# A hybrid decoder step on one core: keys of dilated attention gathered by GpSimd, reciprocal roots as one GpSimd power

## Chip, cores and metric

The kernel runs on one core of one Trainium2 chip. The metric is the device time of one execution in microseconds (us). The engines are called PE (TensorE matmuls; PEld is its weight loads), DVE (VectorE), ACT (ScalarE), POOL (GpSimd) and SP (SyncE, which here issues most DMAs).

## The reference

One layer of a decoder with two mixers side by side, for a prompt of 2048 tokens and for 8 x 8 new tokens ("samples") with cached keys and values. Mixer A is a gated MLP over chunks of 128 positions; mixer B is attention over 8 heads of 64 with three dilated patterns: window 128 with step 1, window 512 with step 4, window 2048 with step 16. The three are mixed by their denominators.

```python
def rms_norm(x, g):
    return x * lax.rsqrt(jnp.mean(x * x, axis=-1, keepdims=True) + EPS) * g

PATTERNS = ((128, 1), (512, 4), (2048, 16))
# project: h = rms_norm(x, g_norm); u, va, za, q, k, vb, zb = split(h @ w_in)
# q, k = rms_norm per head
# dilated_prompt_pattern: query t attends to t - j*r, j = 0..n; keys regrouped into
# r residue classes, blocks of 128 queries against own and previous block of 128 keys
s = jnp.einsum('brnqhd,brnkhd->brnhqk', qb, kb) * SCALE
p = jnp.exp(s - m); o = jnp.einsum('brnhqk,brnkhd->brnqhd', p, vb) / p.sum(-1)
# finish: branches normalised, gated, concatenated, @ w_out, + x; then a gated,
# normalised per-layer embedding is added
```

Every RMS norm needs a reciprocal root per row (per row and head or group in the mixers).

## The kernel before

All products are made in f16 with each operand split in a high and a low half. Eight chunks of the input projection run one after the other in the order A0, B0, B1, A1, B2, B3, A2, A3 (`order`, in the main loop); each takes 16 tiles of 128 tokens and one tile of 64 sample tokens. A tile is one `gemm` (L441): 24 matmuls of 128 x 384 (A) or 128 x 512 (B) columns. Four tiles make a group. `b_evac`/`a_evac` empty the result from PSUM, `b_norm`/`a_norm` normalize a group, with its multiplications on POOL (L500 to L513, L581 and L582).

For a group of mixer B, `b_trans` (L533 to L551) then splits queries and keys of a head pair into halves, and DMA transposes on SP put them into `qk2`, one tile per head pair of 6 x 2048 columns: 64 dimensions times two halves on the 128 partitions. Before, the query blocks hold the high half over the low half, and the keys stand there twice, as high over high (`KH`) and low over low (`KL`).

`attn` queues the units of a head pair. In a group of 512 tokens pattern 1 has four units (one block of 128 queries each) and pattern 2 has four (one residue class each); pattern 3 comes after the fourth group and has eight units of two classes. So a head pair has 40 units. A unit's first half is `scores`: matmuls of 128 queries against 256 keys (128 where there is no previous block) for two heads, twice each (L698 with `KH`, L699 with `KL`); DVE adds the mask and takes the maximum (L704), ACT takes the exponential (L712), DVE splits the result (L715, L716), and a DMA transpose (L718) makes `pT`. Its second half, `stage_c`, multiplies `pT` with the values (L739 to L741). For patterns 2 and 3 queries and keys are slices of `qk2` with a step of 4 and 16 columns, `slice(c + s, T, 16)` for instance: both the stationary operand (queries) and the moving one (keys) are read with that step.

`Pump` spreads the units between the matmuls of `gemm`: it counts time by a cost per matmul and per unit (`scores` returns 4 x blocks x (keys x 0.416 + 8) ns) and releases a unit when the count allows. After that the tile framework orders each engine's instructions by its own estimate of times. Each engine works through its list in order. When a head pair is done, `combine` mixes the three patterns, with ten multiplications and additions on POOL per group of 512 tokens. After the chunks the last stage (`p3_out`, `p3_h`, `p3_gate`, `p3_ple`) makes the outputs tile by tile, and the attention of the samples (`sample`) runs beside it; it multiplies cached keys on POOL (L1126), which wait for loads from the cache.

`rsqrt` (L179 to L191) makes all reciprocal roots: eight DVE instructions, a start value from the bits and two polynomial steps. It is called 115 times, on 1, 4, 8 or 16 columns. Calls stand in `xnorm` (the rows of x, before the first projection), `b_norm`, `a_norm`, `a_mix`, `combine`, `p3_ple`, `sample` and `prep_qk`.

Of the kernel before, what the change touches and what calls it, by code (L numbers as in the profile page):

```python
# [11 lines left out]
F16 = mybir.dt.float16  # L12
F32 = mybir.dt.float32
# [8 lines left out]
P = 128  # L22
# [113 lines left out]
def tile_hymba_gmlp_dilated_attn_step(  # L136
# [42 lines left out]
    def rsqrt(src, n, p=P, mul=1.0):  # L179

        y = small(n, f"rsy{n}")[:p]
        t = small(n, f"rst{n}", 2)[:p]
        nc.vector.tensor_scalar(y.bitcast(I32), src.bitcast(I32), -0.5, MAGIC, op0=ALU.mult, op1=ALU.add)
        nc.vector.tensor_tensor(t, y, y, op=ALU.mult)
        nc.vector.tensor_tensor(t, t, src, op=ALU.mult)
        nc.vector.scalar_tensor_tensor(t, t, -10.0 / 3.0, t, op0=ALU.add, op1=ALU.mult)
        nc.vector.scalar_tensor_tensor(y, t, 5.0, y, op0=ALU.add, op1=ALU.mult)
        nc.vector.tensor_tensor(t, y, y, op=ALU.mult)
        nc.vector.scalar_tensor_tensor(t, t, -0.5 * 0.375 ** 3 * mul, src, op0=ALU.mult, op1=ALU.mult)
        nc.vector.scalar_tensor_tensor(y, t, 1.5 * 0.375 * mul, y, op0=ALU.add, op1=ALU.mult)  # L190
        return y  # L191

    def scales(sg, low):

        sgs = small(1, "sgs")
        nc.vector.tensor_scalar(sgs, sg, 1e-30, None, op0=ALU.max)
        e = small(1, "sge").bitcast(I32)
        nc.vector.tensor_scalar(e, sgs.bitcast(I32), -(2.0 ** -24), MAGIC * 2.0 ** -23, op0=ALU.mult, op1=ALU.add)
        y = small(2, "sgy")
# [11 lines left out]
    ones = cst.tile([P, P], F32, name="ones")  # L211
    nc.gpsimd.memset(ones, 1.0)
    nc.scalar.activation(small(1), ones[:, 0:1], AF.Square)
    mask = cst.tile([P, 2, P], BF16, name="mask")
# [49 lines left out]
    def allsum(col):  # L264
        pt = pst("o", 2)
        nc.tensor.matmul(pt[:, 0:1], lhsT=ones, rhs=col, start=True, stop=True)
        return pt[:, 0:1]
# [65 lines left out]
    def wprep(kind, i, fast=False, room=None):  # L333
# [40 lines left out]
        nc.vector.tensor_scalar(sc[:, 4:5], sc[:, 3:4], VS * VS, None, op0=ALU.mult)  # L374
        yield 0.0
# [24 lines left out]
    def xnorm(j, *behind_):  # L400
# [92 lines left out]
    def b_norm(G, sc, gch):  # L493
# [3 lines left out]
        nc.vector.tensor_scalar(ms[:m, :4 * n], G["ss"][:m, :4 * n], 1.0 / HD, sc[:m, 3:4], op0=ALU.mult, op1=ALU.add)  # L497
        y = rsqrt(ms[:m, :4 * n], 4 * n, m, 2.0 ** 12)
# [33 lines left out]
    def b_trans(G):  # L532
# [3 lines left out]
        for q0 in (0, 2):  # L536

            qkc = wk.tile([P, 2, 768], F16, name=nm("qkc"), tag="hl", bufs=2)
            qv = qkc[:, :, 0:256].rearrange("p j (h c d) -> p j h c d", h=2, c=2)
            k_h = qkc[:, :, 256:512].rearrange("p j (h c d) -> p j h c d", h=2, c=2)  # L540
            k_l = qkc[:, :, 512:768].rearrange("p j (h c d) -> p j h c d", h=2, c=2)
            for q in range(2):
                qs, ks = raw[:, q0 + q, 0], raw[:, q0 + q, 1]
                kd_ = ks.unsqueeze(2).to_broadcast([P, 2, 2, HD])
                nc.scalar.activation(qv[:, q, :, 0, :], qs, AF.Copy)
                nc.scalar.activation(k_h[:, q], kd_, AF.Copy)
                nc.vector.tensor_tensor(qv[:, q, :, 1, :], qs, qv[:, q, :, 0, :], op=ALU.subtract)
                nc.vector.tensor_tensor(k_l[:, q], kd_, k_h[:, q], op=ALU.subtract)
# [5 lines left out]
    def a_group(g, jg, njt, m):  # L554
# [4 lines left out]
        else:  # L559
            t = wk.tile([P, 512], F32, name=nm("sb"), tag="sb", bufs=1)  # L560
# [12 lines left out]
    def a_norm(G, sc, gch):  # L573
# [3 lines left out]
        nc.vector.tensor_scalar(ms[:m, :n], G["ss"][:m, :n], 1.0 / P, sc[:m, 3:4], op0=ALU.mult, op1=ALU.add)  # L577
        y = rsqrt(ms[:m, :n], n, m, 2.0 ** 12 if m == P else 1.0)
# [16 lines left out]
    def a_mix(G, sc, gch):  # L595
# [3 lines left out]
        if m == P:  # L599
# [4 lines left out]
            gg, bb = gch[:, 2, :], bsT  # L604
        else:
            with behind():
                nc.tensor.matmul(pm[:m, 0:P], lhsT=bd8[:, g, :], rhs=G["va"][:m, 0, :], start=True, stop=True)
            gg, bb = gch[:, 1, :], bsS
# [810 lines left out]
```

## Time and profile before

| | |
|---|---|
| median of 3 runs | 1526.23 us (1516.66 to 1528.02) |
| the profiled execution | 1526.24 us, its span 1524.5 us |
| PE busy | 1361.5 us, 89% of the span |
| PEld busy | 693.3 us, 45% |
| DVE busy | 1160.8 us, 76% |
| ACT busy | 725.9 us, 48% |
| POOL busy | 538.1 us, 35% |
| mean granted TensorE clock | 0.959 |

The profile is one execution recorded by the hardware. A group of instructions is named by its line, engine and operation, and by the tiles that it writes and reads (`pss<-qk`: into a PSUM tile for scores, from `qk2`). Matmuls are pipelined, and the recorded durations of neighbours overlap; what a matmul costs in a row of them is the distance from its start to the next one's. A wait is the time for which an engine stood idle before an instruction, put down to what released it last.

### The profile page before, as it was taken

What the parts mean: (1) busy time and instruction counts of PE and PEld (TensorE: products, weight loads), DVE (VectorE), ACT (ScalarE), POOL (GpSimd) and SP (SyncE); (2) the same over time, 40 slices, a digit from 0 to 9 for tenths busy, and PEclk for the clock granted to TensorE, in tenths of its full rate; (3) what the DMA queues carried; (4) which work ended last, traced back from release to release, by engine and by line L of the source; (5) the groups of instructions that cost most, each with busy time, mean ns of one, the idle gap of its engine ahead of it and who ended that gap; (6) DMA issues with size and microseconds to landing.
All of it is one profiled execution on the core that took longest, in us unless ns stands there. A gap on an engine that the chain in (4) does not pass through costs nothing. (4 is left out here: it accounts for less than half of the span.)

```text
span 1524.5 us, 26216 instructions
## 1 busy us (share of the span) xinstructions
PE 1361.5 (89%) x8280; PEld 693.3 (45%) x8280; DVE 1160.8 (76%) x3775; ACT 725.9 (48%) x2083; POOL 538.1 (35%) x547
## 2 busy tenths in 40 slices
PE   2989988997899988899888986788998999899998
PEld 1544544554555434455445643443343344344443
DVE  6777887588988789876999899879756675675555
ACT  6675666565656446655665544754322122221222
POOL 7123122234543654322344356643232330330101
PEclk9999999999999999999999998799999999999999
DMA  7983698588965457977697587876899799796432
GB/s 195 238 181 97 131 176 171 119 176 183 210 155 126 132 120 161 215 142 164 151 211 161 127 207 222 230 204 157 208 224 251 188 255 240 194 242 155 105 94 64
DMA packets 591436, 266.06 MB, mean 175 GB/s; under 512 B 338337, under 2 KB 568801, under 8 KB 591297
## 3 DMA queue, kind: packets, MB, share of 16 engines
q1 hardware_dynamic: 589312, 262.73, 75.4%
q0 software_dynamic: 1984, 1.66, 0.7%
q8 instruction: 65, 1.06, 0.3%
q14 instruction: 75, 0.61, 0.1%
HBM read 134.56 MB, written 48.01 MB: 120 GB/s over the span
## 5 line engine op out<-in xcount | busy, mean ns | idle before, releaser
L441 PE MATMUL psg<-wt,xT 128*128 128x512 f16 (+1 forms) x3072 | 649.6, 367 | 36.5 <-DVE agz L571 15.2
L441 PEld LDWEIGHTS <-xT 128*128 128x128 f16 x3072 | 309.9, 102 | 331.3 <-issue 60.1
L712 ACT ACTIVATE sm<-sm,rec,psc 128x256 f32<-128x256 f32 (+1 forms) x384 | 185.1, 546 | 129.4 <-DVE rec L708 103.1
L698 PE MATMUL pss<-qk 128*128 128x256 f16 (+1 forms) x384 | 132.0, 355 | 31.2 <-DMA qk<-qkc 17.2
L1126 POOL TENSOR_TENSOR K<-K,qB 96x512 f32<-96x512 f32 x64 | 88.4, 1386 | 165.8 <-DMA K<-in_cache_k_dram 70.3
L704 DVE CUSTOM_DVE_ANT_0 sm<-pss,mask 128x256 f32<-128x256 f32 (+1 forms) x384 | 122.7, 360 | 29.2 <-PE pss L699 28.1
L699 PE MATMUL pss<-qk 128*128 128x256 f16 (+1 forms) x384 | 132.8, 358 | 0.0
L874 PEld LDWEIGHTS <-Th 128*128 128x128 f16 x800 | 77.1, 99 | 109.9 <-issue 21.5
L874 PEld LDWEIGHTS <-Tc 128*128 128x128 f16 x800 | 76.4, 98 | 110.6 <-issue 19.9
L716 DVE TENSOR_TENSOR pc<-sm,pc 128x512 f16<-128x512 f32 (+1 forms) x160 | 119.0, 744 | 1.6
L963 POOL TENSOR_TENSOR tg<-tg,x 128x1024 f32<-128x1024 f32 (+1 forms) x16 | 37.6, 2347 | 183.4 <-DVE tg L962 160.4
L874 PE MATMUL psg<-w,Th 128*128 128x512 f16 x400 | 97.6, 387 | 1.2 <-DMA Th<-hl 0.5
L861 ACT ACTIVATE hl<-x,sm 128x1024 f16<-128x1024 f32 (+1 forms) x17 | 19.5, 1147 | 166.0 <-DVE sm L842 140.7
L715 DVE CAST pc<-sm 128x512 f16<-128x512 f32 (+1 forms) x160 | 80.5, 503 | 23.3 <-ACT sm L712 21.3
L874 PE MATMUL psg<-w,Tc 128*128 128x512 f16 x400 | 95.6, 379 | 2.8 <-DMA Tc<-hl 2.8
L874 PE MATMUL pss<-w,Th 128*128 128x512 f16 x400 | 94.9, 379 | 0.0
L874 PE MATMUL pss<-w,Tc 128*128 128x512 f16 x400 | 93.8, 379 | 0.0
L1127 DVE TENSOR_REDUCE blk<-K 96x8 f32<-96x512 f32 x64 | 43.0, 678 | 61.2 <-POOL K L1126 61.1
L776 POOL TENSOR_TENSOR rl<-rl,sm 128x520 f32<-128x520 f32 x48 | 55.7, 1187 | 82.9 <-ACT sm L772 80.0
L739 PEld LDWEIGHTS <-pT 128*128 128x128 f16 x600 | 57.3, 98 | 52.7 <-DMA pT<-pc 43.9
L513 POOL TENSOR_TENSOR gz<-gz,gch 128x512 f32<-128x512 f32 x16 | 20.8, 1301 | 168.9 <-DVE gz L491 83.9
L744 ACT ACTIVATE rec<-pso 128x130 f32<-128x130 f32 (+1 forms) x160 | 44.4, 295 | 46.7 <-PE pso L741 45.3
(324 smaller groups left out, 2649.5 us busy)
## 6 DMA issues: line engine op xcount, KB each, us to landing
K<-in_cache_k_dram SPq DMA_DIRECT2D x64, 192.0 KB
qB<-qd SPq DMA_DIRECT2D x64, 192.0 KB
V<-in_cache_v_dram SPq DMA_DIRECT2D x64, 192.0 KB
vt<-vscr SPq DMA_DIRECT2D x32, 258.0 KB
K<-in_cache_k_dram SPq DMA_DIRECT2D x32, 256.0 KB
V<-in_cache_v_dram SPq DMA_DIRECT2D x32, 256.0 KB
cat<-catd SPq DMA_DIRECT2D x16, 512.0 KB
x<-in_x_prompt_dram SPq DMA_DIRECT2D x16, 512.0 KB
```

The costliest lines, as they stand in the source:

```text
L441: last_mm[0] = nc.tensor.matmul(g[:, :ncol], lhsT=l, rhs=r, start=(n == 0), stop=(n == (23 if j < NT else 15)))
L698: nc.tensor.matmul(pss[:, s, h], lhsT=Q[:, h, qs], rhs=KH[:, h, ks], start=True, stop=False)
L699: nc.tensor.matmul(pss[:, s, h], lhsT=Q[:, h, qs], rhs=KL[:, h, ks], start=False, stop=True)
L704: nc.vector.tensor_tensor_reduce(sm4[:, s, h], pss[:, s, h], mk, 1.0, -3.0e38, op0=ALU.add, op1=ALU.max, accum_out=mx[:, i:i + 1])
L712: nc.scalar.activation(sm4[:, s, h], sm4[:, s, h], AF.Exp, bias=r[:, sl + s, h, HD + 1:HD + 2], scale=psc)
L715: nc.vector.tensor_copy(pc[:, :n], smv)
L716: nc.vector.tensor_tensor(pc[:, n:2 * n], smv, pc[:, :n], op=ALU.subtract)
L739: nc.tensor.matmul(po[:, s, h, 0:65], lhsT=H, rhs=v[:, vs_, a:a + 65], start=(bi == 0), stop=False)
L744: nc.scalar.activation(r[:, sl:sl + ns, :, 0:65], po[:, :ns, :, 0:65], AF.Copy)
L776: nc.gpsimd.tensor_tensor(ti, ti, e[:, i, :].unsqueeze(2).to_broadcast([P, 8, 65]), op=ALU.mult)
L874: last_mm[0] = nc.tensor.matmul(gs[hf], lhsT=o[part][:, kt], rhs=w[:, kt % 2, half, :], start=(n[hf] == 0), stop=(n[hf] == (3 if m == P el ...
L1126: nc.gpsimd.tensor_tensor(K3, K3, qB, op=ALU.mult)
```

## The change

1. `rsqrt` becomes one POOL instruction, `src ** -0.5`, with a constant tile `mhalf`. The factors that the old routine multiplied in are moved into the instructions that make `src`.
2. `b_trans` doubles the queries instead of the keys: `qk2` now holds the query's high half twice (`QH`), its low half twice (`QL`), and the key's high half over its low half (`K`). The two matmuls of a score have the same moving operand and two stationary ones.
3. `gather` copies the keys of patterns 2 and 3 on POOL into tiles `kc` (two buffers), class by class, so that the moving operand's columns follow each other: 512 keys in two instructions, one for each head. For pattern 2 it is queued with the third unit of pattern 1 of the same group; for pattern 3 the first gather is queued with the first unit, the others with the second unit of the gathered group before. A unit of pattern 2 in groups 1 to 3 has its 256 keys in two `kc` tiles, so its matmuls are cut in two of 128 columns. The cost that `scores` returns stays.
4. Small things: `ones` is one column, read with a step of zero; the factor `cS` goes from `gain_load` into `a_mix`; the sample's tile `sb` shares the two buffers of `gz`; some small tiles have fewer buffers.

```diff
-    def rsqrt(src, n, p=P, mul=1.0):
-
+    def rsqrt(src, n, p=P):
         y = small(n, f"rsy{n}")[:p]
-        t = small(n, f"rst{n}", 2)[:p]
-        nc.vector.tensor_scalar(y.bitcast(I32), src.bitcast(I32), -0.5, MAGIC, op0=ALU.mult, op1=ALU.add)
-        nc.vector.tensor_tensor(t, y, y, op=ALU.mult)
-        nc.vector.tensor_tensor(t, t, src, op=ALU.mult)
...
-        nc.vector.scalar_tensor_tensor(y, t, 1.5 * 0.375 * mul, y, op0=ALU.add, op1=ALU.mult)
+        nc.gpsimd.tensor_tensor(y, src, mhalf[:p, :n], op=ALU.pow)
         return y
...
-                kd_ = ks.unsqueeze(2).to_broadcast([P, 2, 2, HD])
-                nc.scalar.activation(qv[:, q, :, 0, :], qs, AF.Copy)
-                nc.scalar.activation(k_h[:, q], kd_, AF.Copy)
...
+                qd_ = qs.unsqueeze(2).to_broadcast([P, 2, 2, HD])
+                nc.scalar.activation(kv[:, q, :, 0, :], ks, AF.Copy)
+                nc.scalar.activation(q_h[:, q], qd_, AF.Copy)
...
-            t = wk.tile([P, 512], F32, name=nm("sb"), tag="sb", bufs=1)
+            t = wk.tile([P, 512], F32, name=nm("sb"), tag="gz", bufs=2)
...
-        Q, KH, KL = qk2[:, 0:2], qk2[:, 2:4], qk2[:, 4:6]
+        QH, QL, K = qk2[:, 0:2], qk2[:, 2:4], qk2[:, 4:6]
+        kc = kcs.setdefault(hp, {})
+
+        def gather(pat, g):
+
+            t = wk.tile([P, 2, 4, P], F16, name=nm("kc"), tag="kc", bufs=2)
+            src = K[:, :, g * 512:(g + 1) * 512].rearrange("p h (i c) -> p h c i", c=4) if pat == 2 else \
+                K.rearrange("p h (i c) -> p h c i", c=16)[:, :, 4 * g:4 * g + 4]
+            for h in range(2):
+                nc.gpsimd.tensor_scalar(t[:, h], src[:, h], 1.0, 1.0, op0=ALU.mult, op1=ALU.mult)
+            kc[pat, g] = t
...
+                if pat == 1 and slot == 2:
+                    gather(2, g)
+                if pat == 3 and (g, slot) == (0, 0):
+                    gather(3, 0)
+                elif pat == 3 and slot and g < 3:
+                    gather(3, g + 1)
...
-                nc.tensor.matmul(pss[:, s, h], lhsT=Q[:, h, qs], rhs=KH[:, h, ks], start=True, stop=False)
-                nc.tensor.matmul(pss[:, s, h], lhsT=Q[:, h, qs], rhs=KL[:, h, ks], start=False, stop=True)
+                n, w = len(ks), kw // len(ks)
+                for i, Q in enumerate((QH, QL)):
+                    for b, k in enumerate(ks):
+                        nc.tensor.matmul(pss[:, s, h, b * w:(b + 1) * w], lhsT=Q[:, h, qs], rhs=keys(h, k),
+                                         start=(i == 0 and b == 0), stop=(i == 1 and b == n - 1))
```

On POOL's list at the start, before the change, the loads of the sample constants (`bsS`, `bd`) stand in a row, and the first arithmetic is the first group's multiplication:

```order
L206 DMA gch_668<-in_g_ob_dram 128x128
L312 DMA bsS<-in_b_s_dram 8x4x1 x8
L317 DMA bd_91<-in_w_s_dram 8x8x1 x4
L292 AFFINE_SELECT w_322<-w_322 128x512
L317 DMA bd_91<-in_w_s_dram 8x8x1 x28
L581 TENSOR_TENSOR agz_331<-agz_331,gch_441 128x512
```

The same place after the change, where the first three powers (L181, for the rows of x) stand between those loads:

```order
L197 DMA gch_566<-in_g_ob_dram 128x128
L305 DMA bsS<-in_b_s_dram 8x4x1 x8
L310 DMA bd_93<-in_w_s_dram 8x8x1 x3
L181 TENSOR_TENSOR sm_158<-sm_155,mhalf 128x1
L310 DMA bd_93<-in_w_s_dram 8x8x1 x2
L285 AFFINE_SELECT w_277<-w_277 128x512
L310 DMA bd_93<-in_w_s_dram 8x8x1 x2
L181 TENSOR_TENSOR sm_185<-sm_182,mhalf 128x1
L310 DMA bd_93<-in_w_s_dram 8x8x1 x16
L181 TENSOR_TENSOR sm_233<-sm_230,mhalf 128x1
```

The first power is behind eleven of the small loads, the second behind fifteen, the third behind thirty-one.

On PE's list, the last unit of pattern 2 of the first head pair before the change, between two projection matmuls (`qk` is the tile `qk2`):

```order
L441 MATMUL psg_3516<-wt_2246,xT_439 128x512
L698 LDWEIGHTS qk_264_1599
L698 MATMUL pss_3379<-qk_264_1599 128x256
L699 LDWEIGHTS qk_264_1599
L699 MATMUL pss_3379<-qk_264_1599 128x256
...
L441 MATMUL psg_3516<-wt_2246,xT_439 128x512
```

After the change, the end of the same unit, and the first unit of pattern 3, which reads a gathered tile for the first time:

```order
L717 MATMUL pss_3175<-kc_2398,qk_236_1378 128x128
L717 LDWEIGHTS qk_236_1378
L717 MATMUL pss_3175<-kc_2846,qk_236_1378 128x128
L435 LDWEIGHTS xT_378
L435 MATMUL psg_3311<-wt_2016,xT_378 128x512
...
L760 MATMUL pso_3161<-vt_3016,pT_3061 128x65
L717 LDWEIGHTS qk_236_1378
L717 MATMUL pss_3204<-kc_3198,qk_236_1378 128x128
```

A unit of pattern 2 has eight matmuls and eight weight loads in place of four; in the piece left out stand 20 projection matmuls and 24 output matmuls.

POOL's list after the change at that place (`kc_2846` holds the last group of pattern 2, the next ones are pattern 3; `gz`, `raw` and `ko` belong to the next chunk's first group):

```order
L651 TENSOR_SCALAR kc_2846<-qk_236_1378 128x512 x2
L181 TENSOR_TENSOR sm_3288<-sm_3286,mhalf 128x16
L651 TENSOR_SCALAR kc_3198<-qk_236_1378 128x512 x2
L651 TENSOR_SCALAR kc_3328<-qk_236_1378 128x512 x2
L507 TENSOR_TENSOR gz_2899<-gz_2899,gch_1642 128x512
L494 TENSOR_TENSOR raw_2896<-raw_2896,sm_3288 128x1024
L651 TENSOR_SCALAR kc_3417<-qk_236_1378 128x512 x2
```

The gathers stand ahead of and between the multiplications of a group's normalization; before the change only the latter stood there.

## Rows read from the trace of the kernel before

**Rows 1.** Busy time by stretch: us, then PE, PEld, DVE, ACT and POOL busy, TensorE clock, DMA.

```profile
110.00:880.00 770.00, 701.71 (x4891) 387.81 (x4890) 634.25 (x2319) 444.16 (x1360) 290.25 (x324) 0.96 0.72 157
880.00:1030.00 150.00, 116.44 (x660) 63.52 (x658) 129.32 (x373) 82.28 (x272) 86.58 (x77) 0.90 0.79 215
...
sum 1524.50, PE 1361.45 PEld 693.31 DVE 1160.79 ACT 725.90 POOL 538.13; mean PE 340.36 PEld 173.33 DVE 290.20 ACT 181.47 POOL 134.53
```

**Rows 2.** What PE waited for, whole span: us in total, times, longest us.

```profile
PE pso L739 <- DMA pT<-pc: 32.1, 23, 4.3
...
PE psg L441 <- DVE agz L571: 15.2, 6, 6.8
PE pss L698 <- DVE sm L704: 13.6, 16, 1.7
PE psg L441 <- DMA xT<-xhl: 10.7, 3, 4.6
```

**Rows 3.** PE in order of time, scores of patterns 1, 2, 3 and 2: start us, us.

```profile
150.06 0.22 PE L699 MATMUL pss<-qk 128*128 128x128 f16 x1
...
150.23 0.38 PE L441 MATMUL psg<-wt,xT 128*128 128x512 f16 x1
...
225.05 0.41 PE L698 MATMUL pss<-qk 128*128 128x256 f16 x1
225.28 0.41 PE L699 MATMUL pss<-qk 128*128 128x256 f16 x1
...
270.09 0.42 PE L698 MATMUL pss<-qk 128*128 128x128 f16 x1
270.33 0.42 PE L699 MATMUL pss<-qk 128*128 128x128 f16 x1
...
328.40 0.30 PE L698 MATMUL pss<-qk 128*128 128x128 f16 x1
328.52 0.29 PE L699 MATMUL pss<-qk 128*128 128x128 f16 x1
```

**Rows 4.** Weight loads in order of time: scores of pattern 2, outputs, scores of pattern 3.

```profile
225.05 0.12 PEld L699 LDWEIGHTS <-qk 128*128 128x128 f16 x1
...
269.54 0.10 PEld L740 LDWEIGHTS <-pT 128*128 128x128 f16 x1
269.56 0.10 PEld L741 LDWEIGHTS <-pT 128*128 128x128 f16 x1
...
270.09 0.14 PEld L699 LDWEIGHTS <-qk 128*128 128x128 f16 x1
```

**Rows 5.** Lines of DVE: costliest and cheapest line of the reciprocal root (busy us, mean ns).

```profile
L184 DVE TENSOR_TENSOR sm<-sm 128x1 f32<-128x1 f32 (+5 forms) x115 | 39.8, 350 | 1.6
...
L188 DVE TENSOR_TENSOR sm<-sm 128x1 f32<-128x1 f32 (+5 forms) x115 | 20.5, 181 | 1.7
```

**Rows 6.** DVE and POOL in order of time around a long small instruction.

```profile
140.84 3.65 DVE L185 TENSOR_TENSOR sm<-sm,sm 64x1 f32<-64x1 f32 x1
...
144.02 0.45 POOL L508 TENSOR_TENSOR raw<-raw,gqk 128x128 f32<-128x128 f32 x1
```

**Rows 7.** Lines of POOL, shapes apart: busy us, mean ns, idle before.

```profile
L778 POOL TENSOR_TENSOR rl<-rl,rl 128x520 f32<-128x520 f32 x32 | 45.1, 1410 | 0.5
L508 POOL TENSOR_TENSOR raw<-raw,gqk 128x128 f32<-128x128 f32 x64 | 36.6, 572 | 0.0
...
L500 POOL TENSOR_TENSOR raw<-raw,sm 128x1024 f32<-128x1024 f32 x16 | 32.2, 2012 | 35.8 <-DVE sm L190 27.3 <-ACT sm L712 3.2 <-DMA out_dram<-vo 2.1
...
L292 POOL TENSOR_SCALAR_AFFINE_SELECT w<-w 128x512 f32<-128x512 f32 x1 | 0.7, 652 | 0.0
...
L1406 POOL MEMSET const-float32-0.0<- 128x1 f32 x1 | 0.1, 99 | 0.3 <-issue 0.3
```

**Rows 8.** The start in order of time, POOL and then DVE.

```profile
15.43 2.23 POOL L317 DMA_DIRECT2D bd<-in_w_s_dram  x4
...
11.38 0.16 DVE L190 SCALAR_TENSOR_TENSOR sm<-sm,sm 128x1 f32<-128x1 f32 x1
```

More of the change, by code (lines that the diff above doesn't have):

```diff
@@ L210, in tile_hymba_gmlp_dilated_attn_step @@
     make_identity(nc, ident)
-    ones = cst.tile([P, P], F32, name="ones")
+    ones = cst.tile([P, 1], F32, name="ones")
     nc.gpsimd.memset(ones, 1.0)
     nc.scalar.activation(small(1), ones[:, 0:1], AF.Square)
+    mhalf = cst.tile([P, 16], F32, name="mhalf")
+    nc.gpsimd.memset(mhalf, -0.5)
     mask = cst.tile([P, 2, P], BF16, name="mask")
@@ L265, in allsum @@
         pt = pst("o", 2)
-        nc.tensor.matmul(pt[:, 0:1], lhsT=ones, rhs=col, start=True, stop=True)
+        nc.tensor.matmul(pt[:, 0:1], lhsT=ones.to_broadcast([P, P]), rhs=col, start=True, stop=True)
         return pt[:, 0:1]
@@ L559, in a_group @@
         else:
-            t = wk.tile([P, 512], F32, name=nm("sb"), tag="sb", bufs=1)
+            t = wk.tile([P, 512], F32, name=nm("sb"), tag="gz", bufs=2)
             ua, gz = t[:, 0:256].unsqueeze(1), t[:, 256:384].unsqueeze(1)
@@ L576, in a_norm @@
         ms = small(4, "ams", 2)
-        nc.vector.tensor_scalar(ms[:m, :n], G["ss"][:m, :n], 1.0 / P, sc[:m, 3:4], op0=ALU.mult, op1=ALU.add)
-        y = rsqrt(ms[:m, :n], n, m, 2.0 ** 12 if m == P else 1.0)
+        f, e = (2.0 ** -24, sc[:m, 5:6]) if m == P else (1.0, sc[:m, 3:4])
+        nc.vector.tensor_scalar(ms[:m, :n], G["ss"][:m, :n], f / P, e, op0=ALU.mult, op1=ALU.add)
+        y = rsqrt(ms[:m, :n], n, m)
         va = G["va"][:m, :n, :]
@@ L640, in tile_hymba_gmlp_dilated_attn_step @@
     v_open = []
+    kcs = {}
     def attn(hp, sc, grp):
@@ L654, in attn @@
                 steps.append((1, n, [(j % 4, j > 0, slice(j * P, (j + 1) * P),
-                                      slice(max(j - 1, 0) * P, (j + 1) * P))]))
+                                      [slice(max(j - 1, 0) * P, (j + 1) * P)])]))
             for c in range(4):
                 steps.append((2, n, [(c, n > 0, slice(n * 512 + c, (n + 1) * 512, 4),
-                                      slice(max(n - 1, 0) * 512 + c, (n + 1) * 512, 4))]))
+                                      [(2, m, c) for m in range(max(n - 1, 0), n + 1)])]))
         rec = {}
@@ L668, in first @@
                 o["r"] = rec[pat]
-                o["pT"], cost = scores(Q, KH, KL, o["r"], sub)
+                keys = lambda h, k: K[:, h, k] if isinstance(k, slice) else kcs[hp][k[0], k[1]][:, h, k[2]]
+                o["pT"], cost = scores(QH, QL, keys, o["r"], sub)
                 return cost
@@ L685, in attn, with scores @@
                 pump.unit(start, comb, None)
-    def scores(Q, KH, KL, r, sub):
+    def scores(QH, QL, keys, r, sub):
         ns = len(sub)
@@ L928, in p3_ple @@
         gs = gemm2(o, 2, wpl, m)
-        s2 = small(2, "es2")
+        s2 = small(2, "es2", 2)
         for hf in range(2):
@@ L932, in p3_ple @@
             nc.scalar.activation(junk[:m], gs[hf][:m], AF.Square, accum_out=s2[:m, hf:hf + 1])
[L933 removed]
+        ic = small(1, "eic", 2)
         nc.vector.tensor_tensor(ic[:m], r[:m], spl[:m, 0:1], op=ALU.mult)
         nc.vector.tensor_tensor(ic[:m], ic[:m], ic[:m], op=ALU.mult)
[L936 removed]
+        ms = small(1, "ems", 2)
         nc.vector.tensor_tensor(ms[:m], s2[:m, 0:1], s2[:m, 1:2], op=ALU.add)
[L938 to L940 removed]
+        nc.vector.tensor_scalar(ms[:m], ms[:m], 4.0 / D, None, op0=ALU.mult)
+        nc.vector.scalar_tensor_tensor(ms[:m], ic[:m], 4.0 * EPS, ms[:m], op0=ALU.mult, op1=ALU.add)
+        y = rsqrt(ms[:m], 1, m)
         e = wk.tile([P, D], F32, name=nm("e"), tag="raw", bufs=2)
@@ L1241, in gain_load @@
     def gain_load(kind, i):
-        gch = wk.tile([P, 3, P], F32, name=nm("gch"), tag="gch", bufs=2)
+        gch = wk.tile([P, 2, P], F32, name=nm("gch"), tag="gch", bufs=2)
         if kind == "B":
```

47 lines of the change are left out of this document (20 added, 27 removed).

## The prediction

> **What bounds the kernel now.** I read three things first: the busy time by stretch [rows 1], what TensorE (PE) stood still for [rows 2], then single instructions in order of time [rows 3 to 6]. In the stretches the reader is to see PE busy for 701.71 of the 770 us in which the attention of the prompt runs between the projections (110 to 880 us). Right after it (880 to 1030 us) VectorE (DVE) is busy for 129.32 of 150 us and PE for 116.44 only. Over all four stretches PE is busy for 1361 of 1524 us and DVE for 1161. So nearly everywhere time follows PE's own work, and the other engines matter where they make PE wait. Its largest wait within the work is for the DMA transposes of the probabilities (32.1 us); two groups of waits for DVE make 15.2 + 13.6 = 28.8 us [rows 2].
>
> The busy figure doesn't say what a matmul costs, since pipelined matmuls overlap; the start of one to the start of the next does. Scores of pattern 1, contiguous on both sides: three of 128 columns between 150.06 and the projection's start at 150.23, so 0.057 us each. Pattern 2, every fourth column: 0.12 us for 128 columns (328.40 to 328.52) and 0.23 us for 256 (225.05 to 225.28). Pattern 3, every sixteenth: 0.24 us for 128 (270.09 to 270.33) [rows 3]. The same columns cost twice and four times as much with a stride. That is what the change goes for.
>
> **Change, part 1: the scores.** Four head pairs. Pattern 2 has 4 groups of 4 units; in groups 1 to 3 a unit holds 4 matmuls of 256 columns (192 in all), in group 0 4 of 128 (64). Pattern 3 has 8 units of 8 matmuls (256). Now: 192 x 0.23 = 44.2, 64 x 0.12 = 7.7, 256 x 0.24 = 61.4, together 113.3 us. Afterwards pattern 2 has 2 x 192 + 64 = 448 matmuls of 128 contiguous columns, pattern 3 256 of them. The queries, now the doubled side, are still strided, so each weight load is still a strided one. A contiguous load takes 0.10 us and loads follow each other every 0.03, so some 0.07 of it is latency that overlaps. The stride-4 load takes 0.12, the stride-16 one 0.14 to 0.15 [rows 4]: less that latency they need 0.05 and 0.075. Pattern 2 is then set by the columns, 448 x 0.057 = 25.5 us, pattern 3 by the loads, 256 x 0.075 = 19.2 us. Gain 113.3 - 44.7 = 68.6 us, all of it on PE in the stretch that PE bounds: **-69**. Ends: all 704 at 0.057 is 40.1 us (-73); a load that hides nothing gives 448 x 0.12 + 256 x 0.145 = 90.9 us (-22). I take the middle case because the loads of the probabilities overlap so plainly.
>
> The Trainium skill's page "SBUF — State Buffer" (section "Door 1: The DMA port swizzle") says that accesses within one 16-byte line run at full rate, so that a step of up to 8 bf16 is free. By that, pattern 2 (8 bytes a step) would gain nothing and the sum would be 26 us smaller. The trace disagrees: 0.12 against 0.057 us for 128 columns. The measurement decides, and the rule has no share in the chances.
>
> **Part 2: reciprocal roots.** Eight DVE lines of 115 instructions each go; they sum to 228.0 us, from 39.8 us for the costliest to 20.5 for the cheapest [rows 5], a fifth of DVE's 1161 us. Little of it stands on PE's path. I give PE back a fifth of its 28.8 us of waits for DVE and of the like small ones: **-8**; ends 0 and all 28.8 us with another 10 of small ones, -39. What replaces them is 115 powers on GpSimd (POOL). No power is in this trace. Below, a POOL instruction on one column takes 0.10 us; above, one on 520 columns takes 1.41 [rows 7]. I take 0.4, nearer to the small one, as a power works on 1 to 16 columns: 46 us over the whole run, on an engine that is busy for 290 of the 770 us. A power ends sooner than eight instructions that DVE mixes with others, so I charge nothing for the hop.
>
> **Part 3: the gathers.** 64 POOL instructions of 512 elements. The nearest one-input row is 0.65 us for 512 columns, the two-input one 1.41 [rows 7]; I take 1.0, so 2.0 us a pair and 64 us in all. With some 70 of the powers POOL comes to about 290 + 64 + 28 = 382 us in a stretch of some 705: not a bound. What counts is whether a pair is ready when PE comes to it. For the first unit of pattern 3 the gather must wait until pattern 2 has last read that buffer, and on PE's list 20 projection matmuls of 512 contiguous columns (4 x 0.057 = 0.23 us each) and output groups stand between: about 4.5 us of cover for 2.0 us. Each of the 32 pairs is charged 0.25 us for the times when POOL is in the middle of something: **+8**; ends 0 and +64 (every pair fully exposed).
>
> POOL's work also reaches DVE. The DVE row at 140.84 us, one column wide, lasted 3.65 us and ended as a string of POOL instructions did (144.02 + 0.45 us) [rows 6]; the cheapest line of its kind takes 0.18 on average [rows 5]. The same page of the Trainium skill (section "Who interferes with whom") says that a DVE instruction with two inputs in SBUF is blocked while a GpSimd instruction reads SBUF; the trace agrees with that. By it 110 us of new POOL work could hold DVE for as long, half of what the roots gave back, and the -8 would be -4. I leave -8, as the roots that go are themselves among the instructions so held.
>
> **Part 4: the start.** The first roots of x now stand on POOL behind the loads of small constants. The list has 8 of one kind and 3 of the next ahead of the first power; in the trace the first of the second kind starts at 15.43 us and four take 2.23 [rows 8], so the first power comes at 17.1 us and its result at 17.5, where DVE's eighth instruction gave it at 11.5. The first matmuls move by up to 6 us. But PE later waits up to 4.6 us for the next tile's transpose [rows 2], whose root is no later than before: the delay goes into that wait. **0**; ends -5 and +5.
>
> **Part 5: what is late next.** With a tenth less PE work in that stretch the transposes of the probabilities come as late as before while PE comes sooner. I add a seventh of the 32.1 us: **+4**; ends 0 and +34. The extra weight loads, the moved factors and the single-column `ones` are inside these figures or worth nothing. The shared buffers (`sb` in the ring of `gz`) can hold up a projection's evacuation; bounded by 0 and 5, taken as 0.
>
> Sum: -69 - 8 + 8 + 0 + 4 = -65. The profiled execution took 1526.24 us, the median of the runs is 1526.23, so nothing is to be corrected: **1461 us**.
>
> **Rivals.** *Weight loads bound* (the strided stationary side takes the place of the strided moving side): -22 - 8 + 8 + 4 = -18, 1508 us. For it: 0.12 and 0.145 us loads; against: those that overlap at 0.03. *The DMA transposes take half of the gain*: -34 in place of -69 and +4, 1526 - 34 - 8 + 8 = 1492 us. For it: the 32.1 us of waits that PE's speed doesn't shorten; against: DVE, from which those transposes get their data, loses a fifth of its work. *Every gather pair exposed by its own 2.0 us*: +64 in place of +8, 1461 - 8 + 64 = 1517 us, no measurable change. *POOL's queue* (the other side): a gather stands behind the normalization of a group, 2.01 for one instruction, eight of 0.57 and one of about 1.3, together 7.9 us of POOL work [rows 7]. With its own 2.0 and 4.5 us of cover it is 5.4 us late, and PE, which works in order, stands that long. If 20 of the 32 pairs fell so, 20 x 5.4 = 108 us: 1461 - 8 + 108 = 1561 us, slower. It decides from about 2.2 us of lateness a pair (69 / 32). For it: one queue, in order; against: a group's normalization stands ahead of its own transposes anyway, and the list has most gathers between such strings.
>
> **How the numbers follow.** Forecast 0.60, transposes 0.12, weight loads 0.13, gathers exposed 0.08, POOL's queue 0.07. A measurement of this kernel tells about 1% (15 us) from no change, 1511 to 1541. The first two and most of the third are faster: 0.82; the exposed gathers and a rest of the third are the same: 0.11; slower: 0.07. The forecast's own range is 1440 to 1485, from -73, -8 and some of the DVE waits on one side and a few us more of each positive term on the other. For 8 in 10 it must take in the transposes and nearly the weight loads: 1437 to 1508.
>
> **What would show it.** In the profile afterwards: scores of pattern 2 every 0.057 us and of pattern 3 every 0.075 (0.12 and 0.145 if the loads bound); the 110 to 880 us stretch shorter by some 60 us at about the same idle time of PE; DVE about 230 us less busy; a power near 0.4 us, a gather near 1.0; PE waits for the gathered keys under 10 us in all. Wrong would be: waits of the scores for POOL of tens of us, a power of several us, projections of the final stage held up by roots behind cache loads on POOL, or the freed time turning up as waits for transposes.

## The result and the profile after

The changed kernel takes 1537.89 us (median of 8 runs, 1532.93 to 1541.07); the kernel before, on the same chip, 1524.61 us (8 runs, 1516.66 to 1529.22). The ratio is 1.0085, 95% interval 1.0058 to 1.0112: slower by 0.9%, about 13 us. The forecast was 1461 us, a gain of 65 us.

Busy time of the profiled execution (busy us, share, instructions):

```profile
span 1536.0 us, 25924 instructions
PE 1315.4 (86%) x8472; PEld 677.0 (44%) x8472; DVE 1050.1 (68%) x2859; ACT 723.4 (47%) x2083; POOL 737.2 (48%) x727
```

PE is busy for 46 us less than before (1361.45, [rows 1]), and the span is 11.5 us longer. So PE's idle time, span less busy, went from 1524.5 - 1361.5 = 163 to 221 us. The stretches (columns as in [rows 1]):

```profile
110.00:880.00 770.00, 655.52 (x5095) 371.55 (x5092) 604.95 (x1931) 445.02 (x1366) 442.87 (x432) 0.93 0.73 157
880.00:1030.00 150.00, 115.26 (x647) 63.07 (x648) 103.26 (x225) 79.69 (x264) 101.87 (x101) 0.87 0.78 211
```

In the first one PE is busy for 46 us less, and its mean granted clock (of 2.4 GHz, the lower level being 1.2) is 0.93 against 0.96, with more idle time between its matmuls. By the clock's record in the two traces the lower level was granted for 126.2 us of the kernel before and for 176.4 us of the changed one; PE was busy for 103.0 and 140.8 us of them. Projection matmuls of 512 columns follow each other every 0.216 us at the higher level and every 0.427 us at the lower. Counted at the higher level, PE's work is therefore about 1310 us before and 1245 us after: it lost 65 us, of which 19 came back through the clock, and 57 us of idle time were added.

POOL has gone from 290 to 443 us in that stretch. The lines of the roots sum to 228.0 us of DVE [rows 5], yet DVE is down by 110.7 only. Two things make the difference. The recorded durations of DVE instructions overlap, so that DVE's other instructions alone were busy for 992.4 us before: without the roots 168 us go and not 228. And these others grew from 992.4 to 1050.1 us.

What PE waited for, whole span, against [rows 2]:

```profile
PE pso L758 <- DMA pT<-pc: 55.9, 41, 3.8
PE pss L717 <- DVE sm L723: 28.6, 21, 3.6
PE psg L435 <- DVE agz L565: 18.9, 6, 6.3
...
PE psg L435 <- DMA xT<-xhl: 17.6, 5, 9.0
```

Each of these lines is longer: the transposes of the probabilities from 32.1 us (23 times) to 55.9 (41), the scores' wait for the mask step from 13.6 to 28.6.

PE in order of time, one run of pattern 2 and one unit of pattern 3, against [rows 3]:

```profile
266.25 1.06 PE L717 MATMUL pss<-kc,qk 128*128 128x128 f16 x16
267.15 4.26 PE L435 MATMUL psg<-wt,xT 128*128 128x512 f16 x19
...
291.82 0.67 PE L717 MATMUL pss<-kc,qk 128*128 128x128 f16 x8
292.32 3.83 PE L435 MATMUL psg<-wt,xT 128*128 128x512 f16 x17
```

Sixteen matmuls in 0.90 us and eight in 0.50: 0.056 and 0.063 us each, where 0.12 and 0.24 stood before. So the scores became as fast as forecast, those of pattern 3 a little faster (0.075 was forecast). Over all of patterns 2 and 3 the distances from start to start (those over 0.4 us counted as 0.4) add up to 113.1 us before and 54.0 after.

POOL's new work, shapes apart (busy us, mean ns, idle time before and its releasers), against [rows 7]:

```profile
L651 POOL TENSOR_SCALAR kc<-qk 128x512 f16<-128x512 f16 x64 | 63.2, 1005 | 72.7 <-DMA qk<-qkc 64.7 <-PE pss L717 8.0
...
L181 POOL TENSOR_TENSOR sm<-sm,mhalf 128x16 f32<-128x16 f32 x16 | 48.5, 3033 | 89.3 <-DVE sm L491 83.0 <-DVE v L466 6.2
...
L181 POOL TENSOR_TENSOR sm<-sm,mhalf 128x1 f32<-128x1 f32 x37 | 22.1, 600 | 59.7 <-DVE sm L401 26.1 <-DVE sm L958 22.2 <-DVE sm L1240 11.0
```

A gather takes the 1.0 us that was estimated. A power does not take 0.4 us: 0.60 on one column, 3.03 on sixteen, 143.6 us for all 115.

The first projection tile and the first power (PE, then POOL), against [rows 8]:

```profile
27.46 6.18 PE L435 MATMUL psg<-wt,xT 128*128 128x384 f16 x24 [8.98 <-DMA xT<-xhl]
...
18.52 0.59 POOL L181 TENSOR_TENSOR sm<-sm,mhalf 128x1 f32<-128x1 f32 x1
```

Before, the first projection started at 22.34 us. From there to the last score it took 852.9 us before (to 875.2) and 854.7 us after (27.46 to 882.2): nothing of the faster scores arrived. From the last projection to the end it took 506 us before and 511 us after.

### The profile page after: what moved, and what is told of

Same layout as the page of the kernel before. It is cut to its first block, busy times and chain, and to the rows that moved or that the text cites. A ratio compares the mean times of both kernels' runs of the same rounds, so it can differ in the third digit from the quotient of the medians.

```text
span 1536.0 us, 25924 instructions
## 1 busy us (share of the span) xinstructions
PE 1315.4 (86%) x8472; PEld 677.0 (44%) x8472; DVE 1050.1 (68%) x2859; ACT 723.4 (47%) x2083; POOL 737.2 (48%) x727
## 4 chain that ended last, share of the span: by engine, by line
PE 38%; DVE 20%; DMA 19%; ACT 8%; issue 6%; SPq 4%; POOL 4%; DVEq 0%; POOLq 0%; ACTq 0%
PE pss L893 11%; PE psg L893 11%; PE psg L435 10%; DMA pT<-pc 3%; DVE sm L723 3%; DVE pc L735 3%; DVE pc L734 2%; ACT sm L731 2%; DMA r3d<-rec 2%; DMA rl<-r2d 2%; DMA K<-in_cache_k_dram 2%; PE pso L1225 2%; DVE rec L727 2%; DMA qk<-qkc 2%; PE pss L717 1%
## 5 line engine op out<-in xcount | busy, mean ns | idle before, releaser
L435 PE MATMUL psg<-wt,xT 128*128 128x512 f16 (+1 forms) x3072 | 659.3, 371 | 50.3 <-DVE agz L565 18.9
L181 POOL TENSOR_TENSOR sm<-sm,mhalf 128x1 f32<-128x1 f32 (+5 forms) x115 | 143.6, 1253 | 242.7 <-DVE sm L491 100.5
L735 DVE TENSOR_TENSOR pc<-sm,pc 128x512 f16<-128x512 f32 (+1 forms) x160 | 127.1, 795 | 2.2
L893 PEld LDWEIGHTS <-Tc 128*128 128x128 f16 x800 | 76.8, 99 | 112.7 <-issue 21.4
L893 PEld LDWEIGHTS <-Th 128*128 128x128 f16 x800 | 77.0, 99 | 108.5 <-issue 21.4
L734 DVE CAST pc<-sm 128x512 f16<-128x512 f32 (+1 forms) x160 | 91.5, 572 | 33.4 <-ACT sm L731 32.2
L717 PEld LDWEIGHTS <-qk 128*128 128x128 f16 x960 | 76.3, 122 | 64.7 <-issue 27.8
L651 POOL TENSOR_SCALAR kc<-qk 128x512 f16<-128x512 f16 x64 | 63.2, 1005 | 72.7 <-DMA qk<-qkc 64.7
L727 DVE TENSOR_SCALAR rec<-sm,nsc 128x2 f32<-128x2 f32 (+1 forms) x160 | 71.2, 462 | 25.4 <-DMA r3d<-rec 11.6
L717 PE MATMUL pss<-kc,qk 128*128 128x128 f16 x704 | 63.7, 234 | 18.4 <-DVE sm L723 18.2
```

Of the source, the lines that this page charges most:

```text
L181: nc.gpsimd.tensor_tensor(y, src, mhalf[:p, :n], op=ALU.pow)
L435: last_mm[0] = nc.tensor.matmul(g[:, :ncol], lhsT=l, rhs=r, start=(n == 0), stop=(n == (23 if j < NT else 15)))
L651: nc.gpsimd.tensor_scalar(t[:, h], src[:, h], 1.0, 1.0, op0=ALU.mult, op1=ALU.mult)
L717: nc.tensor.matmul(pss[:, s, h, b * w:(b + 1) * w], lhsT=Q[:, h, qs], rhs=keys(h, k), start=(i == 0 and b == 0), stop=(i == 1 and b == n - 1))
L727: nc.vector.tensor_scalar(nb, mx[:, :2 * ns].rearrange("p (s h) -> p s h", h=2), nsc, LNP, op0=ALU.mult, op1=ALU.add)
L734: nc.vector.tensor_copy(pc[:, :n], smv)
```

## The experiments

Differences are given to the kernel before as timed on the same chip in the same session (1524.3 to 1526.5 us); the changed kernel stands at +13.3 us. An interval belongs to the ratio to the kernel before.

**Are the powers or the gathers the cost?** Roots on VectorE again, gathers kept (the eight instructions on the same inputs):

```diff
-        nc.gpsimd.tensor_tensor(y, src, mhalf[:p, :n], op=ALU.pow)
+        nc.vector.tensor_scalar(y.bitcast(I32), src.bitcast(I32), -0.5, MAGIC, op0=ALU.mult, op1=ALU.add)
...
+        nc.vector.scalar_tensor_tensor(y, t, 1.5 * 0.375, y, op0=ALU.add, op1=ALU.mult)
```

> The changed kernel with its gathers, but with the reciprocal roots as eight VectorE instructions again. Theory T1 (the 115 powers, 143.6 us of GpSimd work of up to 3.0 us each, are what the gain of the scores is lost to: they come late in GpSimd's queue and stretch VectorE's softmax instructions meanwhile): about 1480 us, 1465 to 1500, GpSimd near 595 us busy, VectorE's copy of the probabilities back near 520 ns. Theory T2 (the units of scores now run as fast as the transposes of the probabilities deliver, whatever the roots cost): 1525 to 1545 us, the waits for transposes stay above 50 us. Theory T4 (the gathers are what costs): 1525 us or more, waits of scores for GpSimd.

1552.18 us, +27.2 (1.0157 to 1.0211). T1 falls: without the powers the kernel is slower still, by 14 us. T2's range ended at 1545, and T4's sign, scores that wait for POOL, does not show. The second kernel keeps the powers and takes `b_trans`, `attn` and `scores` from the kernel before:

> The changed kernel without its gathers: halves, scores and strided keys as before, the roots as GpSimd powers. T1: slower than before by what the scores did not bring, 45 to 65 us, so 1570 to 1590 us. T2: the roots' 228 us off VectorE help or do nothing, 1505 to 1530 us. T4: as T2, 1505 to 1530 us.

1545.47 us, +20.5 (1.0113 to 1.0175): slower, though PE's scores are as before. No theory had that. The gathers on ScalarE:

```diff
-                nc.gpsimd.tensor_scalar(t[:, h], src[:, h], 1.0, 1.0, op0=ALU.mult, op1=ALU.mult)
+                nc.scalar.activation(t[:, h], src[:, h], AF.Copy)
```

> The changed kernel with the 64 gathers on ScalarE instead of GpSimd (63 us of work moved to an engine that is busy for 445 of 770 us), the powers kept. T4 (gathers late in GpSimd's queue, or their port traffic, cost the gain): 1480 to 1500 us. T1: the powers still cost; only the port traffic of the gathers goes, 1520 to 1540 us. T2: no change, 1530 to 1545 us.

1530.38 us, +5.4 (1.0015 to 1.0059): 8 us better than the changed kernel, not the 40 of T4; T1 and T2 both allow it. Each power twice:

```diff
         nc.gpsimd.tensor_tensor(y, src, mhalf[:p, :n], op=ALU.pow)
+        w = small(n, f"rsw{n}", 2)[:p]
+        nc.gpsimd.tensor_tensor(w, src, mhalf[:p, :n], op=ALU.pow)
```

> The changed kernel with each power issued a second time into a scratch tile that nobody reads (144 us more GpSimd work, no more latency for the first result, later for all that stands behind on GpSimd). T1: what one set of powers costs is paid once more, 40 to 60 us, 1580 to 1600 us, with VectorE's copy of the probabilities stretched further from 593 ns. T2 and T4: GpSimd has room (48% busy), 1535 to 1550 us.

1572.33 us, +47.4 (1.0273 to 1.0338), 34 us over the changed kernel and between the ranges of the theories. The page of it:

```profile
PE 1312.3 (84%) x8472; PEld 672.3 (43%) x8472; DVE 1048.2 (67%) x2859; ACT 725.5 (46%) x2083; POOL 873.0 (56%) x842
```

136 us more on POOL, and DVE's 1050.1 became 1048.2: a power does not stretch DVE. Nobody reads the second power, so what it costs must come from what stands behind it in POOL's queue; that is a conclusion, and no run separates it from the new order of the lists. In its waits PE stands for `gz` of mixer B for 21.4 us, against 11.5 in the changed kernel, and for the transposes for 66.1 against 55.9.

**What is the faster score worth by itself?** The kernel before, with contiguous columns of keys, so that its attention leaves out the dilation, and nothing else changed:

```diff
-slice(c + s, T, 16), slice(c + s, T, 16))
+slice(c + s, T, 16), slice((c + s) * P, (c + s + 1) * P))
...
-slice(max(n - 1, 0) * 512 + c, (n + 1) * 512, 4))
+slice(max(n - 1, 0) * 512 + c * P, max(n - 1, 0) * 512 + (c + 1 + (n > 0)) * P))
```

> The kernel before, whose only edit is that patterns 2 and 3 read contiguous keys (the wrong ones, as many columns): no gather, no power, no other instruction anywhere. So it is the PE gain of the scores by itself, with pattern 2's 192 wide matmuls near 0.11 us and pattern 3's at 0.057 to 0.063. T5 (GpSimd's gathers and powers are what eats the gain): 1465 to 1480 us. T2 (PE's list reaches a unit's products with the values earlier, while softmax and transposes take as long as before, so the gain turns into waits and a lower clock): 1510 to 1530 us, waits for transposes of 50 us or more.

1496.27 us, -29.7 (0.9783 to 0.9833), between the two theories. Page and waits:

```profile
span 1494.0 us, 26216 instructions
PE 1298.5 (87%) x8280; PEld 667.9 (45%) x8280; DVE 1161.8 (78%) x3775; ACT 722.7 (48%) x2083; POOL 537.5 (36%) x547
```

```profile
PE pso L739 <- DMA pT<-pc: 58.6, 46, 4.1
PE pss L698 <- DVE sm L704: 20.5, 19, 1.8
```

PE lost 63 us of work (1361.5 to 1298.5) and gained 32 us of idle time, 26.5 of them at the transposes (32.1 to 58.6). Half of the PE gain is lost with no other engine touched: in the two traces the instructions of PE, DVE, ACT and POOL come in the same order to the last one, and the mean clock is 0.961 against 0.959. The way from a unit's last score to its first product with the values fits that: worked out from the starts of these matmuls for all 160 units its median is 16.6 us before, 16.3 here and 16.0 in the changed kernel, while the work between on PE shrank. DVE and ACT need 10.2 to 10.8 us of it (medians, to the end of the subtraction L716 or L735), and where PE waited, 3.9 to 4.3 us more pass from there.

Would more distance on PE's list help? P_LAG, the planner's distance between a unit's halves, from 8000 to 11000, with the contiguous keys and in the changed kernel:

> As the contiguous keys in the kernel before, and the planner's distance between a unit's scores and its products with the values is 11 us instead of 8 (P_LAG): more projection matmuls stand between them on PE's list. T2: part of the gain comes back, 1480 to 1500 us, fewer waits for transposes. T5: no change to the run without the longer distance.

> The changed kernel, gathers and powers kept, P_LAG 11 us instead of 8. T2: 1500 to 1520 us, waits for transposes from 55.9 us to under 35. T5: 1530 to 1545 us, the time is VectorE's and GpSimd's and the order of PE's list does not matter.

1548.3 us, +22.4 (1.0122 to 1.0179), so 52 worse than with the shorter distance; and 1558.06, +32.1 (1.0170 to 1.0233). The remedy fell. The waits for transposes became longer still (with the contiguous keys):

```profile
PE pso L739 <- DMA pT<-pc: 72.3, 53, 2.7
```

The planner lets three units be between their halves (`Pump(3, P_LAG)`), so 11 us of distance admit a unit every 3.7 us at best, 8 us one every 2.7. The waits for transposes grew by 14 us only; PE is also busy for 21 us longer (1319.3 against 1298.5), at a mean clock of 0.936 against 0.961, and the order of the lists is another. That the cap is the reason was not tried; a fourth unit would need one more buffer of `pc` and of `pT` each.

**The roots of the start and of the final stage.** Roots of one column on VectorE (`if n > 1:` ahead of the power, else the eight instructions):

> The changed kernel with the 47 roots of one column (norm of x, final stage, samples) as eight VectorE instructions again, the 68 of 4 to 16 columns as powers. T3 (a root's way through GpSimd's queue delays the chain of the start by 5 us and that of the final stage by 12): 1518 to 1526 us, first projection near 22.5 us instead of 27.5. If those places do not set the end: 1533 to 1542 us.

1531.51 us, +5.6 (1.0014 to 1.0053): 8 us better than the changed kernel, though above T3's range. Its first projection starts at 21.82 us, and from the last projection to the end it takes 502 us instead of 511. T3 holds for these two places; between them the kernel takes some 7 us longer, for which no run gives the reason.

**The shared buffer.** On PE's list of the changed kernel projections wait for `gz` and `agz` where a chunk begins. The kernel before, with only this edit:

```diff
-            t = wk.tile([P, 512], F32, name=nm("sb"), tag="sb", bufs=1)
+            t = wk.tile([P, 512], F32, name=nm("sb"), tag="gz", bufs=2)
```

> The kernel before, whose only edit is that the buffer `sb` of the 64 samples' group is taken from the ring of `gz` (2 buffers) instead of having its own, as in the changed kernel; no instruction differs. Theory T6 (that shared buffer is held from the end of a chunk until the samples' mixing, up to 24 us of planner time later, so the next chunk's second group has only one buffer and its evacuation, and with it PE, stops): 1540 to 1560 us, new waits of projections for VectorE's `gz` and `agz` at the starts of chunks. T5 (the gathers cost the gain): 1520 to 1530 us, no change.

1546.57 us, +20.6 (1.0121 to 1.0160). No instruction was added, and the waits and the place are as expected (waits of PE, PE in order of time, then busy time by stretch as in [rows 1], here and in the kernel before):

```profile
PE psg L441 <- DVE agz L571: 37.9, 8, 11.1
PE pso L739 <- DMA pT<-pc: 25.8, 21, 2.6
...
PE psg L441 <- DVE gz L491: 10.4, 3, 6.9
```

```profile
522.68 10.67 PE L441 MATMUL psg<-wt,xT 128*128 128x512 f16 x38 [6.92 <-DVE gz L491]
533.27 0.43 PE L607 MATMUL pst<-sb,bd 64*64 64x128 f32 x2
...
954.77 0.80 PE L441 MATMUL psg<-wt,xT 128*128 128x384 f16 x2 [11.06 <-DVE agz L571]
```

```profile
520.60:527.20 6.60, 4.52 (x11) 1.66 (x12) 3.38 (x17) 0.85 (x3) 3.27 (x4) 0.50 0.60 164
520.60:527.20 6.60, 6.60 (x33) 2.85 (x31) 4.24 (x16) 2.19 (x8) 3.64 (x4) 1.00 0.68 182
```

The wait for `agz` went from 15.2 us [rows 2] to 37.9. In the wait of 6.92 us for `gz` the granted clock fell to the lower level (0.50), which the kernel before does not show there. Over the span PE has 10 us more idle time (173.0 against 163.0) and is busy for 10 us longer with the same matmuls (1371.4 against 1361.5), at a mean clock of 0.946 against 0.959. The order of the lists changed with the edit too (of PE's 8280 instructions 6237 keep their place), so the 20.6 us are the buffer and the new order together.

The kernel with powers and no gathers has the shared buffer as well, and +20.5 against +20.6 would leave nothing for the powers. But its waits are others: there `agz` and `gz` take 19.9 and 9.0 us, 9 us more than before, where the shared buffer alone makes it 28.5. That one cause explains both runs is not shown; the powers without the shared buffer were not run.

Then the buffer was taken out of the ring: `sb` in `tag="gzl", bufs=1`, with roots on VectorE, in the changed kernel, and with the single-column roots on VectorE:

> Gathers, and roots on VectorE (as in the first run, 1552 us), with `sb` out of the ring of `gz`: it takes the buffer of `gzl`, which only the combination of the patterns uses. T6: 1510 to 1530 us, the jumps at the starts of chunks gone. T5: 1545 to 1555 us, as in the first run.

> The changed kernel with `sb` in the buffer of `gzl`, nothing else. T6: 1505 to 1522 us. T5: 1530 to 1545 us.

> The changed kernel with `sb` in the buffer of `gzl` and the 47 roots of one column on VectorE. T6 with T3: the two gains add, 1498 to 1515 us, faster than before. T5: 1525 to 1535 us, as with the roots alone.

1630.4, 1616.12 and 1609.46 us, +104, +90 and +83: a worse place. In the second of them:

```profile
PE psg L435 <- DVE agz L565: 97.1, 6, 83.8
PE psg L435 <- DVE gz L485: 63.7, 3, 62.6
```

Two single waits of 83.8 and 62.6 us: with one buffer, by the code, the samples wait until `combine` is done with it. These runs say nothing on T6. So `sb` of pattern A's chunks went into another ring, `tag="tmpA" if g < 3 else "gz"`, without and with the single-column roots on VectorE:

> The changed kernel, but in the chunks of pattern A (the last one aside) the samples' `sb` takes a buffer of the ring `tmpA`, which those chunks use for one fold only, instead of one of `gz`. T6 (with the shared buffer alone costing the kernel before 20.6 us): 1515 to 1525 us, the projections' waits for `gz` and `agz` down from 30.4 us to under 20. If in the changed kernel the waits for `gz` come from GpSimd's longer queue instead: 1532 to 1542 us.

> As the run before it in this list, with the 47 roots of one column on VectorE. T6 and T3 add: 1505 to 1520 us, faster than before. Otherwise 1525 to 1535 us, as with the roots alone.

1539.51 us, +13.1 (1.0067 to 1.0117), and 1526.97, +0.5 (0.9988 to 1.0029). The first is no better than the changed kernel, though the waits in question shrank:

```profile
PE pso L758 <- DMA pT<-pc: 65.8, 46, 3.6
...
PE pst L1125 <- ACT KT L1135: 22.9, 4, 7.9
...
PE psg L435 <- DVE agz L565: 7.6, 4, 2.3
PE psg L435 <- DVE gz L485: 7.3, 1, 7.3
```

`gz` and `agz` fell from 30.4 to 14.9 us, the transposes rose from 55.9 to 65.8 and the samples' `KT` from 15.3 to 22.9. A wait removed came back as another. Only a part of the sharing is undone here, since the samples of mixer B and of the last chunk stay in the ring. With the single-column roots on VectorE it is 12.5 us better, but T6 and T3 do not add.

**What do the gathers cost, and the rest?** The changed kernel without gathers, with contiguous keys read from `qk2` and so without the dilation; and with the gather one unit later:

```diff
-                if pat == 1 and slot == 2:
+                if pat == 1 and slot == 3:
```

> The changed kernel without the 64 gathers: patterns 2 and 3 read contiguous keys (the wrong ones, as many matmuls of 128 columns) straight from the transposed tile; doubled queries, powers and shared buffer stay. T5 (the gathers, which stand in GpSimd's queue until the transposes have landed, 64.7 us of waiting, and hold 63 us of its time, cost some 30 us): 1500 to 1515 us. If the rest is the doubled queries and the order of the work: 1530 to 1540 us.

> The changed kernel with pattern 2's gather issued at the fourth unit of pattern 1 instead of the third, so that fewer of the transposes that it waits for are still on the way. T5 by the wait at the head of GpSimd's queue: 1522 to 1532 us, GpSimd's wait of 64.7 us halved. T5 by the gathers' own work and port traffic: no change, 1533 to 1542 us. If the gathers must be early: slower than 1540 us, waits of scores for GpSimd.

1528.69 us, +2.2 (1.0000 to 1.0038): the gathers cost 11 us, not 30. Later gathers: 1535.41, +8.9 (1.0041 to 1.0088), some 4 us better, with POOL's wait at the gathers at 55.8 us instead of 64.7. DVE's busy time without gathers is 1017.0 us, so the 63 us of gathers stretch DVE by 33. With the roots on DVE the difference is 12 us (1174.3 in the first run of this section, 1162.7 in the next one), though there the place of `sb` differs too.

Last, the doubled queries with neither gathers, powers nor shared buffer, and the edits that had helped put together:

> The changed kernel without gathers (contiguous keys, the wrong ones), with all roots on VectorE and `sb` in a buffer of its own: what is left of the change is the doubled queries with matmuls of 128 columns. If these cost nothing: 1492 to 1502 us, as with contiguous keys in the kernel before (1496), and the way from there to the run without gathers (1529) is the shared buffer and the powers. If the doubled queries (twice the strided weight loads, more to transpose late) cost: 1510 to 1530 us.

> Three edits that each did something, together: gathers on ScalarE, the 47 roots of one column on VectorE, `sb` of pattern A's chunks in `tmpA`; the 68 wide roots stay powers. If the 7.5 us of the gathers' move add to the 1527 us of the other two: 1515 to 1523 us, at or a little under the kernel before. If ScalarE's exponentials now stand behind the gathers as GpSimd's work did: 1525 to 1535 us.

The first: 1519.99 us, -4.3 (0.9937 to 0.9986). Of the 29.7 us that contiguous keys gave, doubled queries (with the small edits that came along) leave 4. PE's busy time is 10 us longer than with contiguous keys alone (1308.5 against 1298.5), its idle time 14 (209.2 against 195.5). The scores of patterns 2 and 3, added up as above, take 53.3 us against 49.6, so the doubled loads and the matmuls cut in two slow PE itself by some 4 us. The 10 us go with the clock: it is 0.949 against 0.961, and counted at the higher level PE's work is the same, 1248 against 1250 us. So the loss stands in waits and in the clock. Whether the doubled queries, the small edits or the new order of the lists bring these waits was not tried. The second: 1520.08 us, -4.2 (0.9936 to 0.9990), a kernel that does all of the layer's work and beats the kernel before, by 0.4%.

## Why the prediction was wrong

From the kernel before to the changed one by these runs: contiguous keys -29.7; doubled queries and small edits +25.4 (from -29.7 to -4.3); powers and shared buffer +6.5 (to +2.2); gathers +11.1 (to +13.3). The steps depend on their order, and each but the first also reorders the lists. The shared buffer shows it: 20.6 us alone, and nothing won back in the changed kernel where a part of the sharing was undone.

- **"Gain 113.3 - 44.7 = 68.6 us, all of it on PE in the stretch that PE bounds: -69".** This step failed. The size was nearly right (59 us from start to start); that time follows it was not. PE was busy for 91% of that stretch, but the transposes of the probabilities were already late 23 times. With the same lists on every engine the faster scores gave 29.7 us; in the changed kernel the way from the first projection to the last score is as long as before (854.7 against 852.9 us). The rival in which the transposes take half of the gain was the right one for this part: it put the gain at 34 us, the run at 29.7. The clock, which the sum leaves out, took back 19 us of PE's work in the changed kernel. "Part 5", a seventh of 32.1 us, was mis-sized: they grew by 24 us in the changed kernel, by 26.5 with contiguous keys alone.
- **The extra weight loads and small things are "worth nothing".** Wrong: with the doubled queries they take back 25 us of those 30. This was argued by one sentence and is the largest miss after the first. For the loads themselves it was nearly right (some 4 us on PE's scores); the rest is idle time and a lower clock, and what brings them stays open.
- **The power, 0.4 us.** Wrong: 1.25 us on average, 0.60 to 3.03, the widest above the 1.41 of the upper row. The bound was taken from a row with many columns as though any arithmetic cost the same per column; no row showed a power. "A power ends sooner than eight instructions that DVE mixes with others" failed at the start and in the final stage: with single-column roots on DVE the first projection starts 5.6 us sooner and the final stage is 9 us shorter, and 7.7 and 12.5 us came back in two pairs of runs.
- **DVE relief, -8.** What the powers alone bring is not known: the run without gathers has the shared buffer too (+20.5 against +20.6). With gathers they are worth 14 us (+13.3 against +27.2). The 228 us were too many, since lines were added up whose durations overlap: 168 us of busy time left DVE. In the run with powers and no gathers the other instructions are busy as long as before (994.2 against 992.4), in the changed kernel 58 us longer. Some of the 228 us was time in which POOL held the roots up: against their medians where no POOL instruction overlaps, they took 84 us longer. In the changed kernel the DVE lines that stretched are these:

```profile
L735 DVE TENSOR_TENSOR pc<-sm,pc 128x512 f16<-128x512 f32 (+1 forms) x160 | 127.1, 795 | 2.2
L734 DVE CAST pc<-sm 128x512 f16<-128x512 f32 (+1 forms) x160 | 91.5, 572 | 33.4 <-ACT sm L731 32.2 <-DMA pT<-pc 0.8
L727 DVE TENSOR_SCALAR rec<-sm,nsc 128x2 f32<-128x2 f32 (+1 forms) x160 | 71.2, 462 | 25.4 <-DMA r3d<-rec 11.6 <-DMA r1d<-rec 8.6 <-DMA r2d<-rec 4.6
```

Before, these three took 744, 503 and 353 ns. They stand on the chain from scores to `pT`.

- **Gathers, +8.** The size of one was right (1.0 us). The sum came out near (+11) by luck: it was charged for PE waiting for gathered tiles, and no wait of PE is put down to a gather. What the trace shows of their cost is the 33 us on DVE (12 with the roots there) and the 64.7 us in which POOL's queue stands at a gather for the transposed keys; issued later they cost some 4 us less, on ScalarE some 8.
- **The start, 0.** Wrong: the first power came at 18.52 us (17.1 forecast), the first projection 5.1 us later, and the wait for `xT` grew from 10.7 to 17.6 us in place of taking the delay in.
- **`sb` in the ring of `gz`, "bounded by 0 and 5".** Wrong: 20.6 us alone, the new order of the lists included. Who held the buffer was not read: the samples' mixing is planned 24 us after its chunk (`2 * MIX_LAG`), and the next chunk's evacuation needs the buffer before.

The rival on the slow side (gathers stuck in POOL's queue, 1561 us) had the sign but not the mechanism: scores did not wait for POOL.

## What to carry to other kernels

Before time is taken off the busiest engine, take it off alone, in a kernel that leaves out what the change must pay for it: one run showed that 60 us of PE were worth 30, whatever the rest of the change would do. A buffer that moves into another's ring is an edit with a price; read who holds it longest and who asks next, and try it alone. Where an engine is 90% busy but waits for a chain of others in small pieces, count the chain's latency and the units in flight, since here a removed wait came back as the next one. And busy time of TensorE is to be read with its clock: two kernels with the same matmuls differed by 10 us of busy time.

## What the runs showed of the hardware

A power on POOL took 0.60 us on one column and 3.03 on sixteen, 0.16 us for each further column. It did not slow DVE: a second set of powers, 136 us more on POOL, left DVE at 1048.2 us. Gathers did. The same cast L734 beside a power and beside the second gather of a pair, in the changed kernel:

```profile
169.44 2.92 POOL L181 TENSOR_TENSOR sm<-sm,mhalf 128x16 f32<-128x16 f32 x1 [3.78 <-DVE sm L491]
170.71 0.43 DVE L734 CAST pc<-sm 128x512 f16<-128x512 f32 x1
...
191.27 1.74 POOL L651 TENSOR_SCALAR kc<-qk 128x512 f16<-128x512 f16 x2 [11.27 <-DMA qk<-qkc]
192.42 0.87 DVE L734 CAST pc<-sm 128x512 f16<-128x512 f32 x1
```

Over that trace the cast of 512 columns took 420 ns on average with nothing on POOL (57 times), 423 beside a power alone (21) and 863 beside a gather alone (14); the subtraction L735, which reads two tiles in SBUF, 686, 687 and 1008 ns. The 330 DVE instructions beside nothing but a power took 0.3 us longer in all than their medians without POOL, the 154 beside a gather some 36 us. The Trainium skill's page "SBUF — State Buffer" (section "Who interferes with whom") has a DVE instruction with two inputs in SBUF contend with a GpSimd instruction that reads SBUF. The gathers agree with that; the powers, which read two inputs in SBUF, do not, and here the measurement decides.

Matmuls of 128 columns followed each other every 0.056 us with a stationary operand that was loaded in steps of four columns, and every 0.063 with steps of sixteen, against 0.12 and 0.24 where the moving operand had the step too.
